# Reordering the branch units of a one-core Strassen block: pool, pool, conv, conv, then by turns

## The chip, the cores and the metric

The kernel runs on one core of one Trainium2 chip. The metric is the device time of one execution in microseconds (us), measured over several runs; times are compared by the median. The engines are TensorE (PE, matrix products; PEld are its weight loads), VectorE (DVE), ScalarE (ACT), GpSimd (POOL, which here only issues DMAs and adds by DMA) and SyncE (SP, which issues the loads of the weights).

## The reference

One decoder block over 256 tokens and 4096 channels, in float32. The input is normed and projected by one large matrix; the parts feed a pooling branch and a gated short convolution; both results `ys` (2048 channels each) go through a matrix of their own to 4096 channels, are gated and added, and go through an output matrix.

```python
h = rmsnorm(x, norm_w[l])
proj = jnp.einsum('bsd,de->bse', h, w_in[l])
u_p, z_p, u_c, b_c, c_c, z_c, g_logit = jnp.split(proj, SPLIT_POINTS, axis=-1)
y_pool = causal_multiscale_pool(u_p, pool_w[l], pool_scale[l]) * jax.nn.silu(z_p)
y_conv = causal_gated_shortconv(u_c, b_c, c_c, conv_w[l], conv_b[l]) * jax.nn.silu(z_c)
ys = jnp.stack([y_pool, y_conv], axis=2)
br = jnp.einsum('bsnc,ncd->bsnd', ys, w_branch[l])
gates = jax.nn.sigmoid(g_logit.reshape(b, s, N_BRANCHES, d) + gate_b[l])
merged = jnp.sum(gates * br, axis=2)
x = x + jnp.einsum('bsd,de->bse', merged, w_out[l])
return rmsnorm(x, final_norm_w)
```

## The kernel before

**Units and steps.** The work is a list of units. A unit makes 1024 output columns for all 256 tokens, and works through its input channels in steps of 256 channels. Every operand is split into a high and a low float32r part, and a product is three matmuls: high by high, high by low, low by high. A step is plain (`P`: eight products, 24 matmuls of 128x512) or a Strassen-like step (`S`: seven products, 21 matmuls). The text of a unit, such as `PPPPSSPS`, names its steps in order. Units named `b0_c` and `b1_c` (c from 0 to 3) are the branch units: b0 takes the pooling branch, b1 the convolution, c is the block of 1024 output columns, eight steps each. They come after the gate units (`g1_0` is the last of these) and ahead of the output units `o0` to `o3`.

**Weights.** A step's weights are one load of 1 MB by SP into one of three `raw` buffers; a buffer is loaded again when the step that held it has been prepared. ACT rounds `raw` into the high parts in `ring`, DVE subtracts to make the low parts (`ring<-raw`). For an `S` step DVE also makes four sums in `parts`, which ACT and DVE split the same way (`ring<-parts`). The ring has 15 cells of 512 columns; a plain step takes 4, an `S` step 3 and then 4 more. PE gives a cell back when its products are done. Work is written out up to four steps ahead of PE, three at the end of a unit that is marked urgent, and each engine runs its instructions in the order in which they are written.

**Banks.** Four PSUM banks (`sums`) hold the output quarters and four more (`shared`) the corners of the `S` steps. When a bank has its last matmul, ACT empties it: `sums` into `E`, `shared` into `J`. DVE combines the corners in `J` and adds them to `E` (`E<-E,J`). In a unit that is marked `late`, POOL adds them instead by two accumulating DMAs (`gather`, E<-J). In a plain last step the `sums` banks close in its second half; in a closing `S` step they close in its first nine matmuls, and one in the step before.

**What follows a unit.** `epi` returns a list of actions, of which one is written out per tick, a tick being six matmuls of PE; `gap(n)` is n empty ticks. For `b0_c` the result in `E` is multiplied by its gate in `Y` (`Y<-E,Y`). For `b1_c` `E` is multiplied by the gate in the tile `last_pair`, which `spare()` returns (`gated`), then the product of the first branch is added; PE transposes the sum into `shared`, ACT copies it, and POOL stores it in `m_d[c]` (`put`). `Y` then takes the next gate from `gates_d`. The first two gates are never stored: `g0_0` lies in `Y`, `g1_0` in `last_pair`.

**Fills.** The operands of the branch units (`y_ops`) come from DRAM (`y_d`) through three staging tiles `sa`, `sb`, `sc`, into `arena`: POOL fetches, DVE makes four small sums for an `S` operand, ACT writes the high part, DVE the low (`arena<-sa` and so on). They start in the last gate unit, first all of b0 in the order of its steps, then all of b1; the output units' operands follow from `m_d` in the same way, each once its c has been stored.

Lines 58 and 61 of the profile are the helpers for ACT and DVE, 82 and 85 those of POOL's DMAs, 1026 the matmuls of steps and 462 the transposes.

Of the kernel before, what the change touches and what calls it, by code (L numbers as in the profile page):

```python
# [9 lines left out]
F32 = mybir.dt.float32  # L10
# [5 lines left out]
P = 128  # L16
# [3 lines left out]
NU = 1024  # L20
NH = 512
# [19 lines left out]
HOST = "PPBPPMMPSSPSSPSSPSS"  # L41
TEN = "PSPSSPSSPSSPSSPS"
OUT3 = "PSPSPSPSPSPSSPPP"
B0 = "PPPPSPSP"
B1 = "PSPSPSPP"
B1_FIRST = "PPSPSPSP"
B0_MORE = "PPPPSSPS"


@with_exitstack  # L50
def hybrid_block(ctx: ExitStack, tc: tile.TileContext, x, xc, prm, rows_in, w_in, pool_w, w_branch, w_out, out):
# [5 lines left out]
    def act(dst, src, func=AF.Copy, **kw):  # L57
        return pin(nc.scalar.activation(dst, src, func, **kw))  # L58

    def tt(dst, a, b, op):  # L60
        return pin(nc.vector.tensor_tensor(out=dst, in0=a, in1=b, op=op))  # L61

    def mul(dst, a, b):
        return tt(dst, a, b, ALU.mult)

    def add(dst, a, b):
        return tt(dst, a, b, ALU.add)
# [13 lines left out]
    def move(dst, src):  # L81
        return pin(nc.gpsimd.dma_start(dst, src))
# [8 lines left out]
    dram = ctx.enter_context(tc.tile_pool(name="dram", bufs=1, space=bass.MemoryType.DRAM))  # L91

    def sb(name, shape, dt=F32):
        return upper.tile(shape, dt, name=name)

    def blocks(name, shape, dt=F32):
        return const.tile(shape, dt, name=name)
# [4 lines left out]
    E = blocks("E", [P, 2, NU])  # L102
    sa = blocks("sa", [P, 8, P])
    J = blocks("J", [P, 4, NH])
    ident = blocks("ident", [P, P])
    raw = sb("raw", [P, NRAW, 2 * NU])
    Y = sb("Y", [P, 2, NU])
# [10 lines left out]
    gates_d = dram.tile([2, 4, P, 2, NU], F32, name="gates_d")  # L118
    g_d = dram.tile([2, P, 2, NU], F32, name="g_d")
    side_d = dram.tile([2, P, 2, 4, P], F32R, name="side_d")  # L120
    y_d = dram.tile([2, 2, P, 4, 2, T], F32, name="y_d")
    m_d = dram.tile([4, P, 4, 2, T], F32, name="m_d")
    o_d = dram.tile([3, P, 2, NU], F32, name="o_d")

# [28 lines left out]
    def open_last(dt):  # L153
        stack = ExitStack()
        ctx.enter_context(stack)
        pool = stack.enter_context(tc.tile_pool(name="last", bufs=1, side="right"))
        last_pair.update(stack=stack, tile=pool.tile([P, 8 * KB], dt, name="last_pair"))
# [87 lines left out]
    def quarters(tile_):  # L245
        return tile_.rearrange("p a (b c) -> p (a b) c", c=NH)
# [154 lines left out]
    def shared(i):  # L401
        return PF[i]
# [52 lines left out]
    def transposes(src, done):  # L455
        items = []
        for j in range(4):
            def f(j=j):
                for i in range(2):
                    for t in range(2):  # L460
                        c = (2 * j + i) * P
                        pin(nc.tensor.transpose(shared(j)[:, i * T + t * P:i * T + (t + 1) * P],  # L462
                                                src[:, t, c:c + P], ident))
                done(j)
            items.append(f)
        return items

    def pairs(items):
        return [lambda a=a, b=b: (a(), b()) for a, b in zip(items[::2], items[1::2])]

    def put(dst, src):
        for k in range(2):
            move(dst[:, :, 1 - k], src.rearrange("p (q k) t -> p q k t", k=2)[:, :, k])

    def chan(tile_):
        return tile_.rearrange("p a n -> p (a n)").rearrange("p (b t) -> p b t", t=T)

    def bankview(j):
        return shared(j).rearrange("p (b t) -> p b t", t=T)

    def gap(n):
        return [None] * n
# [36 lines left out]
    def seq_y(text):  # L519
        return sequence(text, 8 - text.count("S"), 8, 0)  # L520
# [189 lines left out]
    def spare():  # L710
        return last_pair["tile"].rearrange("p (a n) -> p a n", a=2)

    def branch_unit(n, c):
        def epi(u):
            if n == 0:
                if c:
                    return gap(10) + [lambda: move(spare(), gates_d[1, c])] + gap(8) + [lambda: mul(Y, E, Y)]
                return gap(8) + [lambda: mul(Y, E, Y)]
            turned = spare() if c < 3 else Y

            def gated():
                mul(E, E, spare())
                if c == 3:
                    last_pair["stack"].close()
                    open_last(F32R)
                    last_pair["again"] = True

            def copy(j):
                act(chan(turned)[:, 2 * j:2 * j + 2], bankview(j))

            def stored():
                put(m_d[c], chan(turned))
                merged[c] = now[0] + STORED
            return gap(2) + [gated, None, lambda: add(E, E, Y), None,
                lambda: c < 3 and move(Y, gates_d[0, c + 1])] + gap(4) + pairs(transposes(E, copy)) + [stored]

        text = (B1 if c else B1_FIRST) if n else B0_MORE if c else B0
        u = Unit(f"b{n}_{c}", lambda i: w_branch[n, c, i], seq_y(text), y_ops[n], epi)
        u.late = n == 0 and c > 0
        if not u.late:  # L740
            u.urgent, u.lead = (lambda: None), 3
        units.append(u)
# [91 lines left out]
            gate_unit(n, c)  # L834
    gate_unit(1, 0)
    last_x = units[-1]
    for c in range(4):
        branch_unit(0, c)
        branch_unit(1, c)
    for c in range(4):  # L840
        out_unit(c)

# [126 lines left out]
    def done(i):  # L969
        steps[i].prepared = True  # L970
# [184 lines left out]
    for st in lead:  # L1155
# [7 lines left out]
        if not combined and last.closed(FB):  # L1163
            combined = True
            flush()
            rest = sums.rearrange("p (t a) n -> p t (a n)", t=2)
# [80 lines left out]
```

## Time and profile before

| what | value |
|---|---|
| runs | 2356.61, 2357.35, 2359.06 us; median 2357.35 |
| profiled execution | 2356.82 us, span 2354.7 us |
| granted TensorE clock, mean | 0.999 |
| branch units, from the first to the last matmul | 1674.9 to 2014.3 us of the span |
| matmuls and transposes | 10424 |
| DMA | 569.44 MB, mean 242 GB/s |

The page counts an engine's busy time; PE's matmuls overlap in the pipeline, so that the busy time of a group is not its count times its pitch. "Idle before" is how long the engine stood ahead of an instruction, and the name behind the arrow is what ended that. In a table by windows each row is a stretch of the span, with the busy time and the number of instructions of PE, PEld, DVE, ACT and POOL, then PE's granted clock, the DMA engines' share and GB/s. In a timeline each row is a start, a duration and the work, and equal neighbours are merged.

### The profile page before, as it was taken

To read this page: it belongs to the slowest core of one execution; us is meant where nothing else is said; L and a number is where in the kernel's file an instruction comes from. 1 tells how busy PE (TensorE), PEld (TensorE's weight loads), DVE (VectorE), ACT (ScalarE), POOL (GpSimd) and SP (SyncE) were. 2 spreads that over 40 slices of the span, in tenths; PEclk is the share of its full clock that TensorE was granted. 3 is DMA by queue.
4 is the path that set the end of the run, shared out by engine and by line. 5 is a ranking of instruction groups with operands and counts; after the bars stand their busy time and mean duration, and the time that the engine had idled before them with its cause. 6 is when DMAs were issued, how large, how long until landed. Compare 5 with 4: busy or idle time off the path is not lost.

```text
span 2354.7 us, 28337 instructions
## 1 busy us (share of the span) xinstructions
PE 2340.7 (99%) x10424; PEld 1938.7 (82%) x10424; DVE 2217.8 (94%) x2454; ACT 1542.9 (66%) x1841; POOL 139.0 (6%) x195
## 2 busy tenths in 40 slices
PE   9999999999999999999999999999999999999998
PEld 7888888888888888888888888888888888888886
DVE  8899989999979979979999999998999899999998
ACT  6666756766656666666677767677666566566664
POOL 0000000000001000100000000001101001000000
PEclk9999999999999999999999999999999999999999
DMA  9667655776656656656787787778767678767877
GB/s 351 231 234 248 217 201 215 251 232 233 222 207 216 219 196 213 220 198 222 242 258 254 256 265 246 250 267 283 258 225 247 254 247 282 250 206 263 260 255 279
DMA packets 95387, 569.44 MB, mean 242 GB/s; under 512 B 10320, under 2 KB 10576, under 8 KB 34832
## 3 DMA queue, kind: packets, MB, share of 16 engines
q1 hardware_dynamic: 69824, 485.39, 56.7%
q0 software_dynamic: 24848, 81.01, 13.7%
q8 instruction: 81, 1.33, 0.2%
q10 hardware_dynamic: 576, 1.24, 0.1%
q14 instruction: 58, 0.48, 0.1%
HBM read 521.46 MB, written 25.17 MB: 232 GB/s over the span
## 4 chain that ended last, share of the span: by engine, by line
PE 97%; DVE 1%; DMA 0%; ACT 0%; issue 0%; DVEq 0%; SPq 0%; ACTq 0%
PE sums L1026 70%; PE shared L1026 25%; PE shared L676 1%; PE shared L462 1%; DVE ring L61 1%; DMA raw<-in_w_branch_dram 0%; DVE parts L61 0%; DMA raw<-in_w_in_dram 0%; ACT ring L58 0%; DVE arena L61 0%; PE shared L652 0%; DVE J L61 0%; ACT E L58 0%; PE shared L653 0%; PE shared L655 0%
## 5 line engine op out<-in xcount | busy, mean ns | idle before, releaser
L1026 PE MATMUL sums<-ring,arena 128*128 128x512 f32 x7011 | 1640.7, 390 | 1.9 <-ACT E L58 1.1
L1026 PEld LDWEIGHTS sums<-ring,arena 128*128 128x128 f32 x7011 | 1315.3, 188 | 275.5 <-ACT E L58 1.5
L61 DVE TENSOR_TENSOR ring<-raw,ring 128x1024 fp32r<-128x1024 f32 (+2 forms) x887 | 962.2, 1104 | 70.4 <-ACT ring L58 69.5
L58 ACT ACTIVATE ring<-raw 128x1024 fp32r<-128x1024 f32 (+3 forms) x682 | 785.5, 1192 | 210.2 <-PE sums L1026 98.5
L58 ACT ACTIVATE ring<-parts 128x512 fp32r<-128x512 f32 (+1 forms) x683 | 510.4, 761 | 510.2 <-DVE parts L61 438.3
L1026 PE MATMUL shared<-ring,arena 128*128 128x512 f32 x2241 | 541.1, 389 | 0.0
L61 DVE TENSOR_TENSOR ring<-parts,ring 128x1024 fp32r<-128x1024 f32 (+1 forms) x475 | 524.5, 1146 | 8.7 <-ACT ring L58 8.7
L1026 PEld LDWEIGHTS shared<-ring,arena 128*128 128x128 f32 x2241 | 420.6, 188 | 87.3
L61 DVE TENSOR_TENSOR parts<-parts,raw 128x512 f32<-128x512 f32 x444 | 303.3, 683 | 0.0
L61 DVE TENSOR_TENSOR parts<-raw 128x1024 f32<-128x1024 f32 x222 | 270.2, 1217 | 10.9 <-DMA raw<-in_w_in_dram 6.0
L61 DVE TENSOR_TENSOR J<-J 128x512 f32<-128x512 f32 (+1 forms) x90 | 78.1, 868 | 6.0 <-ACT J L58 2.8
L1026 PE MATMUL sums<-ring,last_pair 128*128 128x512 f32 x306 | 76.2, 389 | 0.0
L58 ACT ACTIVATE J<-shared 128x512 f32<-128x512 f32 x128 | 69.5, 601 | 1.6
L1026 PEld LDWEIGHTS sums<-ring,last_pair 128*128 128x128 f32 x306 | 57.4, 188 | 11.9
L85 POOL DMA_DIRECT2D E<-J x28 | 34.2, 1463 | 479.5 <-ACT ring L58 300.1
L1026 PE MATMUL shared<-ring,last_pair 128*128 128x512 f32 x216 | 51.9, 389 | 0.0
L1026 PE MATMUL shared<-ring,side 128*128 128x512 f32 x207 | 50.7, 389 | 0.0
L1026 PEld LDWEIGHTS shared<-ring,last_pair 128*128 128x128 f32 x216 | 40.5, 188 | 8.4
L1026 PEld LDWEIGHTS shared<-ring,side 128*128 128x128 f32 x207 | 38.9, 188 | 8.1
L58 ACT ACTIVATE E<-sums 128x512 f32<-128x512 f32 x76 | 41.8, 592 | 4.5 <-PE sums L1026 2.7
L85 POOL DMA_DIRECT2D Y<-J x12 | 14.7, 1458 | 265.1 <-ACT ring L58 138.5
L58 ACT ACTIVATE E<-sums,rin 128x512 f32<-128x512 f32 x20 | 13.0, 689 | 13.9 <-PE sums L1026 13.9
(140 smaller groups left out, 645.6 us busy)
## 6 DMA issues: line engine op xcount, KB each, us to landing
raw<-in_w_in_dram SPq DMA_DIRECT2D x318, 1024.0 KB, 4.9
raw<-in_w_branch_dram SPq DMA_DIRECT2D x64, 1024.0 KB, 5.4
raw<-in_w_out_dram SPq DMA_DIRECT2D x64, 1024.0 KB, 4.8
E<-J POOLq DMA_DIRECT2D x28, 512.0 KB, 8.6
E<-in_rows_dram POOLq DMA_DIRECT2D x14, 512.0 KB, 9.8
Y<-J POOLq DMA_DIRECT2D x12, 512.0 KB, 9.3
gates_d<-E POOLq DMA_DIRECT2D x6, 1024.0 KB, 6.1
y_d<-E POOLq DMA_DIRECT2D x8, 512.0 KB, 5.2
```

The source lines that it names most:

```text
L58: return pin(nc.scalar.activation(dst, src, func, **kw))
L61: return pin(nc.vector.tensor_tensor(out=dst, in0=a, in1=b, op=op))
L85: return pin(nc.gpsimd.dma_start(dst, src, accum_op=ALU.add))
L462: pin(nc.tensor.transpose(shared(j)[:, i * T + t * P:i * T + (t + 1) * P], src[:, t, c:c + P], ident))
L676: pin(nc.tensor.matmul(o, a, b, start=(k, i) == (0, 0), stop=(k, i) == (3, 2)))
L1026: pin(nc.tensor.matmul(ps, lhs, rhs, start=n == 0, stop=n == u.total[b] - 1))
```

## The change

The order of the branch units was b0_0, b1_0, b0_1, b1_1, and so on by turns. Now it is b0_0, b0_1, b1_0, b1_1, and from c = 2 by turns. Two products of the first branch then wait at the same time, and there is one `Y`: the first goes to DRAM (`p_d`), `Y` takes the gate of the second, and after b1_0 the first comes back into `J`, where it is added. `last_pair` gets the gate of b1_1 only after m_d[0] has been stored from it.

All b0 units have the text `PPPPSSPS` and are late. b0_0 had `PPPPSPSP` and was not late. b1_0 had `PPSPSPSP` and now has `PSPSPSPP`, as all b1 units but b1_1, which has `PPPPSSSP`.

```diff
-B0 = "PPPPSPSP"
 B1 = "PSPSPSPP"
-B1_FIRST = "PPSPSPSP"
-B0_MORE = "PPPPSSPS"
+B_LATE = "PPPPSSPS"
+B1_SECOND = "PPPPSSSP"
...
+    p_d = dram.tile([P, 2, NU], F32, name="p_d")
...
             if n == 0:
-                if c:
-                    return gap(10) + [lambda: move(spare(), gates_d[1, c])] + gap(8) + [lambda: mul(Y, E, Y)]
-                return gap(8) + [lambda: mul(Y, E, Y)]
+                product = gap(18) + [lambda: mul(Y, E, Y)]
+                if c == 0:
+                    return product + [None, lambda: move(p_d, Y), lambda: move(Y, gates_d[0, 1])]
+                if c > 1:
+                    product[10] = lambda: move(spare(), gates_d[1, c])
+                return product
...
-            return gap(2) + [gated, None, lambda: add(E, E, Y), None,
-                lambda: c < 3 and move(Y, gates_d[0, c + 1])] + gap(4) + pairs(transposes(E, copy)) + [stored]
-
-        text = (B1 if c else B1_FIRST) if n else B0_MORE if c else B0
+            head = gap(2) + [gated, None, lambda: add(E, E, Y), None,
+                             lambda: c < 3 and move(Y, gates_d[0, c + 1])] + gap(4)
+            rest = []
+            if c == 0:
+                head = [lambda: move(J, p_d.rearrange("p a (b n) -> p (a b) n", n=NH)), None, gated] + gap(4) + [
+                    lambda: add(quarters(E), quarters(E), J)] + gap(3)
+                rest = gap(7) + [lambda: move(spare(), gates_d[1, 1])]
+            return head + pairs(transposes(E, copy)) + [stored] + rest
+
+        text = B_LATE if n == 0 else B1_SECOND if c == 1 else B1
         u = Unit(f"b{n}_{c}", lambda i: w_branch[n, c, i], seq_y(text), y_ops[n], epi)
-        u.late = n == 0 and c > 0
+        u.late = n == 0
...
-    for c in range(4):
-        branch_unit(0, c)
-        branch_unit(1, c)
+    for n, c in ((0, 0), (0, 1), (1, 0), (1, 1), (0, 2), (1, 2), (0, 3), (1, 3)):
+        branch_unit(n, c)
```

The instructions of an engine stand in a fixed order. Three places of it matter below.

DVE in the second half of b0_0, before: the lows and sums for the seventh step (`S`) and the lows of the last one (`P`), with pieces of fills between.

```order
L61 TENSOR_TENSOR parts<-raw 128x1024
L61 TENSOR_TENSOR ring<-raw,ring 128x512
L61 TENSOR_TENSOR parts<-parts,raw 128x512
L61 TENSOR_TENSOR ring<-raw,ring 128x2x512
L61 TENSOR_TENSOR parts<-parts,raw 128x512
L61 TENSOR_TENSOR arena<-sb,arena 128x1024
L61 TENSOR_TENSOR ring<-parts,ring 128x2x512 x2
L61 TENSOR_TENSOR arena<-sc,arena 128x512
L61 TENSOR_TENSOR ring<-raw,ring 128x2x512 x2
L61 TENSOR_TENSOR sa<-sa 128x128 x4
L61 TENSOR_TENSOR ring<-raw,ring 128x4x512
```

The same place now: the last lows of the sixth step, the lows of the seventh (`P`), and then all of the last one, which is an `S`.

```order
L60 TENSOR_TENSOR arena<-sa,arena 128x1024
L60 TENSOR_TENSOR ring<-parts,ring 128x2x512
L60 TENSOR_TENSOR ring<-parts,ring 128x512 x2
L60 TENSOR_TENSOR ring<-raw,ring 128x2x512 x2
L60 TENSOR_TENSOR arena<-sb,arena 128x512
L60 TENSOR_TENSOR sc<-sc 128x128 x4
L60 TENSOR_TENSOR parts<-raw 128x1024
L60 TENSOR_TENSOR ring<-raw,ring 128x512
L60 TENSOR_TENSOR parts<-parts,raw 128x512
L60 TENSOR_TENSOR ring<-raw,ring 128x2x512
L60 TENSOR_TENSOR parts<-parts,raw 128x512
L60 TENSOR_TENSOR ring<-parts,ring 128x2x512 x2
```

Where one plain step was being prepared stands a Strassen step; the fills between are of about the same size.

POOL from the last fetches of `y_d` on, before:

```order
L82 DMA sc<-y_d 128x512
L82 DMA sa<-y_d 128x512
L82 DMA Y<-gates_d 128x2048
L82 DMA m_d<-last_pair 512x1x256 x2
L82 DMA sa<-m_d 128x512
L82 DMA sb<-m_d 128x512
L82 DMA sc<-m_d 128x512
L85 DMA E<-J 128x2x512 x2
L82 DMA last_pair<-gates_d 128x2048
```

And now:

```order
L81 DMA sc<-y_d 128x512
L81 DMA sa<-y_d 128x512
L84 DMA E<-J 128x2x512 x2
L81 DMA p_d<-Y 128x2048
L81 DMA Y<-gates_d 128x2048
L84 DMA E<-J 128x2x512 x2
L81 DMA J<-p_d 128x2048
L81 DMA m_d<-last_pair 512x1x256 x2
L81 DMA sa<-m_d 128x512
L81 DMA sb<-m_d 128x512
L81 DMA last_pair<-gates_d 128x2048
```

Two adding DMAs for b0_0, the store of `p_d` and the load from it are new; the first store into `m_d` stands behind them.

DVE after b1_0, before: the corners are added to `E`, then the gate is applied, and the product in `Y` is added between the sums of a Strassen step and their lows.

```order
L61 TENSOR_TENSOR E<-E,J 128x2048
L61 TENSOR_TENSOR ring<-raw,ring 128x4x512
L61 TENSOR_TENSOR E<-E,last_pair 128x2048
L61 TENSOR_TENSOR parts<-raw 128x1024
L61 TENSOR_TENSOR ring<-raw,ring 128x512
L61 TENSOR_TENSOR parts<-parts,raw 128x512
L61 TENSOR_TENSOR ring<-raw,ring 128x2x512
L61 TENSOR_TENSOR parts<-parts,raw 128x512
L61 TENSOR_TENSOR E<-E,Y 128x2048
L61 TENSOR_TENSOR ring<-parts,ring 128x2x512 x2
```

And now, in b1_1, which follows b1_0:

```order
L60 TENSOR_TENSOR E<-E,J 128x2048
L60 TENSOR_TENSOR ring<-raw,ring 128x4x512
L60 TENSOR_TENSOR E<-E,last_pair 128x2048
L60 TENSOR_TENSOR parts<-raw 128x1024
L60 TENSOR_TENSOR ring<-raw,ring 128x512
L60 TENSOR_TENSOR parts<-parts,raw 128x512
L60 TENSOR_TENSOR ring<-raw,ring 128x2x512
L60 TENSOR_TENSOR parts<-parts,raw 128x512
L60 TENSOR_TENSOR E<-E,J 128x2048
L60 TENSOR_TENSOR ring<-parts,ring 128x2x512 x2
```

The product is added at the same place, from `J` in place of `Y`; the second `E<-E,J` is the one that reads what came back from `p_d`. PE's transposes of `E` stand 69 matmuls into the unit that follows b1_0, as before.

## The prediction

> **What bounds the kernel now.** I read the page first, then what TensorE (PE) waited for, then the branch stage by windows, then the timelines at the places that the change touches. PE does 99% of the span and 97% of the chain that ended last.
>
> ```profile
> span 2354.7 us, 28337 instructions
> ...
> PE 2340.7 (99%) x10424; PEld 1938.7 (82%) x10424; DVE 2217.8 (94%) x2454; ACT 1542.9 (66%) x1841; POOL 139.0 (6%) x195
> ...
> PE 97%; DVE 1%; DMA 0%; ACT 0%; issue 0%; DVEq 0%; SPq 0%; ACTq 0%
> ```
>
> A busy PE could still be a slow PE, so the pitch of the matmuls is wanted: in the first row below 26 matmuls start between 1769.70 and 1775.60 (the next row's start), 0.227 us each. The waits of PE come to 3.0 us in three places, two of them at the very start of the program. The third lies in the stage that is changed.
>
> ```profile
> 1769.70 6.06 PE L1026 MATMUL sums<-ring,arena 128*128 128x512 f32 x26
> 1775.60 1.03 PE L462 MATMUL shared<-ident,E 128*128 128x128 f32 x8
> ...
> PE shared L873 <- DVE warm L869: 1.1, 1, 1.1
> PE sums L1026 <- ACT E L58: 1.1, 1, 1.1
> PE sums L1026 <- DVE ring L774: 0.8, 1, 0.8
> ```
>
> The four windows below are the first four branch units (b0_0, b1_0, b0_1, b1_1). Only the first loses PE time. VectorE (DVE) is nearly full in the first two, where the operands of both branches are still being filled, and has room in the next two.
>
> ```profile
> 1674.90:1718.30 43.40, 42.33 (x188) 34.72 (x186) 41.67 (x51) 31.21 (x39) 5.06 (x8) 1.00 0.80 263
> 1718.30:1760.00 41.70, 41.70 (x184) 34.51 (x185) 40.74 (x44) 27.32 (x34) 0.00 (x0) 1.00 0.55 202
> 1760.00:1803.20 43.20, 43.20 (x200) 35.95 (x199) 39.45 (x38) 26.24 (x32) 3.64 (x6) 1.00 0.71 255
> 1803.20:1844.70 41.50, 41.50 (x184) 34.36 (x184) 37.67 (x35) 27.14 (x32) 3.05 (x3) 1.00 0.75 255
> ```
>
> So a gain is bounded: PE cannot run ahead of its own matmuls, and there is one wait to take away. What is open is whether DVE, which feeds PE, is still in time.
>
> **The change part by part.**
>
> *One Strassen step more in the first unit.* A plain step is 24 matmuls, a Strassen step 21. Before, b0_0 holds two of them, now three; every other unit keeps three. Three matmuls fewer at 0.227 us: -0.7 us, straight on PE.
>
> *The wait at the end of b0_0.* It comes from ScalarE (ACT):
>
> ```profile
> 1710.95 6.28 PE L1026 MATMUL sums<-ring,arena 128*128 128x512 f32 x27
> 1718.30 1.90 PE L1026 MATMUL sums<-ring,arena 128*128 128x512 f32 x7 [1.07 <-ACT E L58]
> ...
> 1715.76 1.49 ACT L58 ACTIVATE ring<-raw 128x1536 fp32r<-128x1536 f32 x1 [1.29 <-DMA raw<-in_w_branch_dram]
> 1717.15 0.61 ACT L58 ACTIVATE arena<-sb 128x512 fp32r<-128x512 f32 x1
> 1717.67 2.04 ACT L58 ACTIVATE E<-sums 128x512 f32<-128x512 f32 x4
> ```
>
> After 27 matmuls from 1710.95 the next was due at 1717.08 and came at 1718.30: 1.2 us, and 0.1 more in the slower start of the second row. ACT stood at the rounding of a weight tile that had not landed, and the emptying of the sums banks was queued behind it. The unit ended with a plain step, whose banks close in the last 2.7 us. Now it ends with a Strassen step, which closes one bank in the step before and the others in its first nine matmuls, as b0_1 does before, at whose end (1803.20) the windows show no loss. -1.3 us. This is gone unless DVE is late there, which is the next term.
>
> *DVE in b0_0.* The rows are those of before, from the first sum of its fifth step:
>
> ```profile
> 1687.48 1.21 DVE L61 TENSOR_TENSOR parts<-raw 128x1024 f32<-128x1024 f32 x1
> ...
> 1691.56 1.22 DVE L61 TENSOR_TENSOR arena<-sc,arena 128x1024 fp32r<-128x1024 f32 x1
> 1692.69 2.35 DVE L61 TENSOR_TENSOR ring<-parts,ring 128x1024 fp32r<-128x1024 f32 x2
> 1694.97 0.68 DVE L61 TENSOR_TENSOR arena<-sa,arena 128x512 fp32r<-128x512 f32 x1
> 1695.57 1.01 DVE L61 TENSOR_TENSOR sb<-sb 128x128 f32<-128x128 f32 x4
> 1696.50 2.35 DVE L61 TENSOR_TENSOR ring<-raw,ring 128x1024 fp32r<-128x1024 f32 x2
> 1698.77 1.22 DVE L61 TENSOR_TENSOR parts<-raw 128x1024 f32<-128x1024 f32 x1
> ...
> 1698.03 2.88 PE L1026 MATMUL shared<-ring,arena 128*128 128x512 f32 x12
> ```
>
> By start to start: the five sums and lows of a Strassen step 1691.56 - 1687.48 = 4.08, its last two lows 2.28, a plain step's lows 2.27, fills 1.13 (1024 wide), 0.60 (512), four small sums 0.93; a fill 896 wide lies between, I take 1.0. In the new order, from the same 1687.48: sums 4.08 (1691.56), three fill pieces 1.0 + 0.60 + 0.93 (1694.09), lows 2.28 (1696.37), the next step's sums 4.08 (1700.45), a fill 1.13 (1701.58), lows in three pieces, about 2.34 (1703.92), a plain step 2.27 (1706.19), 0.60 + 0.93 (1707.72), the last step's sums 4.08 (1711.80) and lows 2.28 (1714.08). PE: the fifth step starts six matmuls before 1698.03, at 1696.67; then 21, 21 and 24 matmuls bring the last step to 1711.65. Its third group (in a closing step N4, on the last of the four summed cells) needs its low part seven matmuls in, at 1713.24. DVE is 0.85 us late there, +0.85; up to there it is in time, by 0.5 us at the narrowest. Bounds: 0 if the fills run shorter, and 0.85 + 1.7 = 2.6 if DVE also idles as it did in that window (43.40 - 41.67). I take 0.85: the rows of before had hardly any idle time inside this stretch.
>
> *After it.* The fills of the second branch (five of the eight still stand here) and the sums of b0_0 now lie beside b0_1, which has four plain steps first. Summed the same way, DVE ends the lows of b0_1's last step about 1.5 us before PE needs them. +0.1, bounds 0 and 2.6 - 1.5 = 1.1.
>
> *E by way of DMA in b0_0.* Its corner sums are now added by two accumulating DMAs and not by DVE. That takes one 2.29 us add from DVE and puts two transfers into b0_1, 9.5 us each by the median in the fence after the next paragraph, 19 us if one followed the other; their reader, the product Y<-E,Y, stands 18 ticks of six matmuls, 24.5 us, behind. Hidden by b0_1's own matmuls: 0.
>
> *Y to p_d and back.* After that product POOL stores Y and, once it has landed, loads the next gate into Y. Behind these two on POOL's queue stand only the adding DMAs of b0_1, due at the end of the unit; two transfers of some 6 us fit. No PE work waits for them: 0. Back comes the product into J, and here something does wait. These rows of before show the same place one unit pair on (b1_1 to b0_2, unit start 1844.7):
>
> ```profile
> 1845.56 2.29 DVE L61 TENSOR_TENSOR E<-E,J 128x2048 f32<-128x2048 f32 x1 [0.46 <-ACT E L58]
> 1856.73 2.28 DVE L61 TENSOR_TENSOR E<-E,Y 128x2048 f32<-128x2048 f32 x1
> 1860.38 1.03 PE L462 MATMUL shared<-ident,E 128*128 128x128 f32 x8
> 1859.33 0.56 POOL L82 DMA_DIRECT2D Y<-gates_d  x1 [47.35 <-DVE E L61]
> ...
> raw<-in_w_branch_dram SPq DMA_DIRECT2D x35, 1024.0 KB, 5.5
> Y<-gates_d POOLq DMA_DIRECT2D x3, 1024.0 KB, 5.6
> E<-J POOLq DMA_DIRECT2D x4, 512.0 KB, 9.5
> last_pair<-gates_d POOLq DMA_DIRECT2D x2, 1024.0 KB, 17.6
> ```
>
> J may be loaded once E<-E,J has read it, at +3.1; issue took 0.3 us more for Y (1859.33 against 1859.01). With 5.6 us J lands at +9.1. The adding of J has the place that E<-E,Y had, +12.0, and PE's transposes come at +15.7. So 2.9 us of room at the add, and 4.2 us (15.7 - 9.1 - 2.3 for the add is 4.3, less the semaphores) until PE stands: 0. Bound above: 17.6 us, the same size behind two adding DMAs; it is the rival below. I take 5.6, since the two DMAs ahead of J landed long before.
> [...]
>
> *Three Strassen steps in a row in b1_1.* The ring of 15 cells lets a third step (7 cells) in only as the first gives its cells back, so DVE cannot work far ahead; but the four plain steps before leave it in front. At the end of b1_1 a plain step closes the banks late again, with three weight tiles of the next unit emitted ahead of the emptying: the pattern of the old wait. Bounds 0 (the end of b1_1 in before, 1844.70) and 1.3 (the end of b0_0 in before). DVE frees the weight tile earlier than in b0_0, without fills: I take 0.3.
>
> *Later units.* The cells of the ring shift by three, and the transposes come three matmuls later; both only move pieces: 0.
>
> Sum: -0.7 - 1.3 + 0.85 + 0.1 + 0.3 = -0.75 us. The profiled execution took 2356.82 us (span 2354.7 and 2.1 around it), 0.53 below the median 2357.35; so 2356.1 for its like, and 2356.6 as a median.
>
> **The rivals.**
>
> *A. Everything is covered.* The two gains stand alone: 2357.35 - 2.0 = 2355.35. For it: b0_1 to b1_3 of before ran with no PE wait at all. Against: DVE is 96% full in the very window that gets 4.1 us more DVE work (6.36 for a Strassen step against 2.27).
>
> *B. DVE is the bound through the first two units.* The upper bounds together: -2.0 + 2.6 + 1.1 + 1.3 = +3.0, 2360.35. For it: the windows at 41.67 and 40.74 busy. Against: PE needs 183 matmuls per unit and the fills that are left for the second unit stand beside four plain steps in a row.
>
> *C. J comes late (the other side).* The transposes of E stand in PE's order behind the add of J. From a landing time of about 9.9 us (4.3 more than 5.6) on, each further us is one of PE. At 17.6 us, J lands at +21.0, the add ends at +23.4, PE stands 7.7 us: 2356.6 + 7.7 = 2364.3, slower by 0.3%; it passes the 4.7 us line at a landing of some 15.4 us. For it: the 17.6 us row, for the same size on the same queue. Against: that row stood behind E<-J, and nothing stands ahead of J here.
> [...]
>
> *D. The order is not what it says.* The instruction order shows all three moves and one Strassen step more; the time would be 2357.35. Hardly open.
>
> **How the numbers follow.** Forecast (one small wait in b0_0, the rest hidden) 0.55; A 0.20; B 0.14; C 0.08; D and others 0.03. 0.2% is 4.7 us, about what a measurement of this kernel can tell from no change. The forecast, A, B and D lie within it. Faster by more would need a gain over the 2.0 us that PE has to give: 0.02. Slower: C and a B beyond its bound, 0.09. Same: 0.89. The range reaches from A, less 0.4 for the scatter of runs (the runs of before lie between 2356.61 and 2359.06), to B: 2355.0 to 2360.3.
>
> **What would show it.** In the changed profile: no ACT wait of PE at the end of b0_0; instead, if anything, about a us in its last step, released by DVE's ring lows. J<-p_d landing 5 to 7 us after its issue, the second E<-E,J of DVE without idle time before it, and the transposes of b1_1 without a wait. A PE stop at those transposes would be C; PE waits spread over b0_0 and b0_1 would be B; a PE wait on ACT at the end of b1_1 above 1 us would make the 0.3 wrong.

## The result, and the profile after

The changed kernel took 2360.59 us (median of 20 runs, 2359.86 to 2363.72) against 2357.15 us for the kernel before in the same session (20 runs, 2355.99 to 2360.21). The ratio is 1.0016, 95% interval [1.0010, 1.0022]: 3.4 us slower, where 0.75 us faster was forecast, and just outside the range. The profiled execution took 2361.99 us, 1.4 above its median; the last section takes that up. One execution each of e4_tick, e6_text_only, e10_two_s_lead2 and e12_j_twice took more than 3000 us, in the slow state, and is left out of the medians below.

The page of the changed kernel answers to the first fence of the prediction: span, TensorE's busy time, and the shares of the chain that ended last.

```profile
span 2360.3 us, 28353 instructions
...
PE 2341.0 (99%) x10421; PEld 1937.3 (82%) x10421; DVE 2220.6 (94%) x2460; ACT 1543.6 (65%) x1845; POOL 142.4 (6%) x199
...
PE 97%; DMA 1%; DVE 1%; ACT 0%; issue 0%; SPq 0%; DVEq 0%; ACTq 0%
```

The three matmuls are gone (10421 for 10424), but the span is 5.6 us longer. What PE waited for, over the whole execution:

```profile
PE sums L1034 <- ACT E L57: 3.0, 2, 1.9
PE sums L1034 <- DVE ring L60: 2.1, 2, 1.8
...
PE sums L1034 <- DVE arena L60: 1.1, 1, 1.1
```

The two rows left out, and the 1.8 of the second, stand at the program's start. In the branch units PE now waits twice for ScalarE's emptying of `E` (once before) and once for `ring` (the 0.3 that is left of that row), and in the output unit o0 once for `arena`. By windows, the first and the fourth unit in their new order (b0_0 and b1_1):

```profile
1675.20:1718.57 43.37, 41.99 (x185) 34.10 (x183) 41.61 (x55) 29.35 (x36) 4.36 (x7) 1.00 0.68 224
...
1801.96:1847.33 45.37, 43.46 (x201) 35.82 (x199) 38.01 (x33) 26.40 (x30) 4.23 (x7) 1.00 0.73 266
```

The first unit loses 1.4 us, the fourth 1.9; the two between them lose nothing. There are four places to look at.

**The last step of b0_0 and its end.** PE's timeline, and below it ScalarE's over the same place:

```profile
1707.63 6.05 PE L1034 MATMUL sums<-ring,arena 128*128 128x512 f32 x26
1714.00 0.74 PE L1034 MATMUL sums<-ring,arena 128*128 128x512 f32 x2 [0.32 <-DVE ring L60]
1714.58 2.93 PE L1034 MATMUL shared<-ring,arena 128*128 128x512 f32 x12
1718.57 3.77 PE L1034 MATMUL sums<-ring,arena 128*128 128x512 f32 x14 [1.06 <-ACT E L57]
```

```profile
1713.15 2.08 ACT L57 ACTIVATE ring<-raw 128x1024 fp32r<-128x1024 f32 x3
1715.13 0.62 ACT L57 ACTIVATE arena<-sa 128x512 fp32r<-128x512 f32 x1
1715.65 0.58 ACT L57 ACTIVATE E<-sums 128x512 f32<-128x512 f32 x1
1716.13 1.90 ACT L57 ACTIVATE ring<-raw 128x2048 fp32r<-128x2048 f32 x1
1717.94 1.55 ACT L57 ACTIVATE E<-sums 128x512 f32<-128x512 f32 x3
```

From 1707.63 and 26 pitches of 0.227 the next matmul was due at 1713.53 and came at 1714.00: VectorE was late with a low part. From 1714.58 and 12 pitches b0_1 was due at 1717.30 and came at 1718.57. ScalarE had emptied one `sums` bank at 1715.65, then rounded a whole weight tile for b0_1 (1.90 us), and only then emptied the other three.

**The end of b1_1.** PE, ScalarE and the DMAs from 1828 to 1848 (count, size, median us from issue to landing):

```profile
1839.14 6.28 PE L1034 MATMUL sums<-ring,arena 128*128 128x512 f32 x27
1847.33 8.92 PE L1034 MATMUL sums<-ring,arena 128*128 128x512 f32 x31 [1.91 <-ACT E L57]
```

```profile
1840.17 1.92 ACT L57 ACTIVATE ring<-raw 128x2048 fp32r<-128x2048 f32 x1 [1.59 <-DMA raw<-in_w_branch_dram]
1841.99 1.06 ACT L57 ACTIVATE J<-shared 128x512 f32<-128x512 f32 x2
1844.88 1.91 ACT L57 ACTIVATE ring<-raw 128x2048 fp32r<-128x2048 f32 x1 [1.82 <-DMA raw<-in_w_branch_dram]
1846.70 2.04 ACT L57 ACTIVATE E<-sums 128x512 f32<-128x512 f32 x4
```

```profile
raw<-in_w_branch_dram SPq DMA_DIRECT2D x4, 1024.0 KB, 7.9
last_pair<-gates_d POOLq DMA_DIRECT2D x1, 1024.0 KB, 10.9
...
sc<-m_d POOLq DMA_DIRECT2D x1, 256.0 KB, 12.3
```

b0_2 was due at 1839.14 + 27 x 0.227 = 1845.26 and came at 1847.33: 2.07 us. ScalarE stood at the rounding of b0_2's third weight tile, whose load had not landed, with the emptying of all four banks queued behind it. The loads, 5.5 us by the median before, took 7.9 here, beside four fetches by POOL. Of the 31 matmuls that follow, eight near the start stand 0.427 us apart in place of 0.227, which is another 1.6 us.

**The last step of o0.** PE and VectorE:

```profile
2098.94 0.61 PE L1034 MATMUL sums<-ring,arena 128*128 128x512 f32 x2
2100.62 1.88 PE L1034 MATMUL sums<-ring,arena 128*128 128x512 f32 x7 [1.06 <-DVE arena L60]
```

```profile
2099.48 1.08 DVE L60 TENSOR_TENSOR arena<-sa,arena 128x896 fp32r<-128x896 f32 x1
```

VectorE writes the last piece of the step's own operand at 2099.48 to 2100.56; PE was due at 2098.94 + 2 x 0.227 = 2099.39.

**The way by DRAM.** The tile `J` and the add that reads it:

```profile
L81 POOL DMA_DIRECT2D J<-p_d x1: 567/567/567, 1805.4 to 1805.4; - x1
...
DMA to landing us min/median/max: 5.1/5.1/5.1
```

```profile
1813.96 2.29 DVE L60 TENSOR_TENSOR E<-E,J 128x2048 f32<-128x2048 f32 x1
...
1817.61 1.03 PE L462 MATMUL shared<-ident,E 128*128 128x128 f32 x8
```

Issued at 1805.39, landed at 1810.46, read at 1813.96 without idle time ahead of the add; the transposes come at 1817.61 without a wait.

The table sums what PE lost against its pitch of 0.227 us at each place, read from the starts of its matmuls, for this and for the kernels of the next section (from b0_0 on; the start of o0, at most 0.32 us, and losses below 0.3 are left out; "end of the second unit" is where b1_0 ends in the old order). Slow matmuls are in the number. The transposes in b0_2 have no column; e8_all and e10_two_s_lead2 lose about 0.5 there.

| kernel | in b0_0 | end of b0_0 | b0_1 | end of the second unit | transposes in b1_1 | end of b1_1 | end of o0 | o2 |
|---|---|---|---|---|---|---|---|---|
| before | | 1.35 | | | | | | 0.31 |
| after | 0.59 | 1.62 | | | | 3.77 | 1.33 | |
| e1_lead2 | 0.58 | 1.67 | | | | | 1.32 | |
| e2_fetch_later | 0.58 | 1.67 | | | | | 1.32 | |
| e3_sss_pp | 0.58 | 1.66 | | | 2.4 | 0.49 | 1.32 | |
| e4_tick | 0.58 | 1.67 | | | | 4.52 | | 0.59 |
| e5_limit | 0.59 | | 1.73 and 1.68 | | | 1.59 | 1.34 | |
| e6_text_only | | 1.58 | | 2.20 | | | 1.34 | |
| e7_two_s | | | | | | 4.15 | | |
| e8_all | 0.59 | | 1.70 and 0.53 | | | | | 0.40 |
| e9_j_late | 0.59 | 1.62 | | | | 2.30 | 1.34 | |
| e10_two_s_lead2 | | | | | | | | |
| e11_before_held | | | | 1.49 | | | | |
| e12_j_twice | 0.58 | 1.65 | | | 1.2 | 3.90 | 1.33 | |

For the changed kernel: 7.31 less the 1.66 of before, less 0.68 for the three matmuls, is 5.0; with 0.24 at the start of o0 and 0.3 by which b0_0 begins later that is 5.5 of the span's 5.6.

### The profile page after: what moved, and what is told of

It is laid out like the page before. It is cut to its first block, busy times and chain, and to the rows that moved or that the text cites. A ratio compares the mean times of both kernels' runs of the same rounds, so it can differ in the third digit from the quotient of the medians.

```text
span 2360.3 us, 28353 instructions
## 1 busy us (share of the span) xinstructions
PE 2341.0 (99%) x10421; PEld 1937.3 (82%) x10421; DVE 2220.6 (94%) x2460; ACT 1543.6 (65%) x1845; POOL 142.4 (6%) x199
## 3 DMA queue, kind: packets, MB, share of 16 engines
q8 instruction: 81, 1.33, 0.2%
## 4 chain that ended last, share of the span: by engine, by line
PE 97%; DMA 1%; DVE 1%; ACT 0%; issue 0%; SPq 0%; DVEq 0%; ACTq 0%
PE sums L1034 70%; PE shared L1034 25%; PE shared L676 1%; PE shared L462 1%; DMA raw<-in_w_in_dram 1%; DVE ring L60 0%; DMA raw<-in_w_branch_dram 0%; ACT ring L57 0%; PE shared L652 0%; PE shared L653 0%; PE shared L655 0%; ACT E L57 0%; ACT arena L57 0%; SPq L75 0%; DVE parts L60 0%
## 5 line engine op out<-in xcount | busy, mean ns | idle before, releaser
L60 DVE TENSOR_TENSOR parts<-parts,raw 128x512 f32<-128x512 f32 x446 | 308.5, 692 | 0.0
```

## The experiments

Each edit is against the changed kernel unless it says otherwise.

### Two tiles ahead at the end of b1_1

```diff
-            u.urgent, u.lead = (lambda: None), 3
+            u.urgent, u.lead = (lambda: None), 2 if c == 1 else 3
```

> At the end of b1_1 (the fourth unit) two weight tiles of the next unit are rounded by ACT ahead of the emptying of the sums banks, not three. Theory Q (the emptying is queued on ACT behind the rounding of the third tile, whose load lands late): the PE stop of 2.07 us between b1_1 and b0_2 goes, and with it the eight matmuls at 0.427 us that follow it (1.6 us in the changed kernel's profile): 2 to 3.7 us faster than the changed kernel, about 2357.5. Rival S (three Strassen steps in a row leave DVE and ACT behind as a whole): the stop stays at 1 us or more, because the banks or the next tiles are late anyway, and the time stays within 1 us of the changed kernel.

2358.45 us (before: 2356.76; ratio 1.0008, [0.9999, 1.0017]), span 2356.2. ScalarE and PE at the end of b1_1:

```profile
1843.11 2.64 ACT L57 ACTIVATE E<-sums 128x512 f32<-128x512 f32 x4 [1.57 <-PE sums L1034]
```

```profile
1838.83 13.54 PE L1034 MATMUL sums<-ring,arena 128*128 128x512 f32 x59
```

ScalarE now waits for the banks and not for a load, with the third tile behind the emptying, and 59 matmuls run through. The stop and the slow matmuls are gone, all else is unchanged. The order in ScalarE's queue is a necessary condition of that stop.

### The fetches for o0 later

```diff
-                merged[c] = now[0] + STORED
+                merged[c] = now[0] + STORED + (24 if c == 0 else 0)
```

> The three fetches from m_d[0] that follow its store are issued 24 ticks later, so that they no longer share the DMA engines with the loads of the weights in the last third of b1_1; the load of the gate into last_pair stays. Theory D (the third tile is late because its load shares the engines with these fetches: 8.5 us against 4.7 us undisturbed): the load takes 5 to 6.5 us and the stop between b1_1 and b0_2 shrinks by 2 us or more, to nothing. Rival R (the raw buffer is free too late, whatever the load takes): the stop shrinks by less than 1 us.

2358.41 us (ratio 1.0007, [0.9998, 1.0016]), span 2356.5. The weight loads of the same window, and ScalarE's third tile, which keeps its place ahead of the emptying:

```profile
raw<-in_w_branch_dram SPq DMA_DIRECT2D x4, 1024.0 KB, 5.1
```

```profile
1842.38 1.92 ACT L57 ACTIVATE ring<-raw 128x2048 fp32r<-128x2048 f32 x1
1844.18 2.06 ACT L57 ACTIVATE E<-sums 128x512 f32<-128x512 f32 x4
```

Without the three fetches of `m_d` beside them the loads take 5.1 us in place of 7.9, ScalarE no longer waits, and the stop is gone as well. So it took both: a tile ahead of the emptying, and a load that POOL's fetches made late. Either mend alone is enough.

### The three Strassen steps one place earlier in b1_1

```diff
-B1_SECOND = "PPPPSSSP"
+B1_SECOND = "PPPSSSPP"
```

> b1_1 has its three Strassen steps still in a row, but one place earlier (PPPSSSPP). Theory E (what matters is that a Strassen step stands just before the closing plain step, so that the raw buffers and ring cells for the next unit come free late): the stop between b1_1 and b0_2 goes, as at the end of b1_1 before; 2 to 3.7 us faster than the changed kernel, unless the transposes, which now stand beside the first of the three, cost up to 1 us. Rival S (three in a row are the cause): a stop of 1 us or more stays, there or inside the three steps.

2362.51 us (ratio 1.0023, [1.0014, 1.0033]). The stop at the end shrinks to 0.49, but there is a new one among PE's waits, and VectorE's add, in its timeline, shows why:

```profile
PE shared L462 <- DVE E L60: 2.2, 1, 2.2
```

```profile
1818.14 2.28 DVE L60 TENSOR_TENSOR E<-E,J 128x2048 f32<-128x2048 f32 x1
```

The sums of the second Strassen step now come ahead of the adding of `J` in VectorE's order; `J` was issued at 1805.9 and with the 5.1 us of above had landed at about 1811, but the add ran from 1818.14 to 1820.42, and PE's transposes waited for it. The time in which VectorE adds `J` is set by its own queue, not by the transfer. Two plain steps at the end shrink one stop by making another.

### One half tick more

```diff
     for u in units:
+        if u.name == "b0_1":
+            state["mm"] += 3
```

> The count that makes the ticks gets three more at the start of b0_1, so that all later actions fall at the same matmul of their unit as before the change. Theory T (the three matmuls that the first unit lost shift every later tick; by that the last fill of o0 slid behind the lows of one more step): the PE stop of 1.2 us before the last step of o0 goes, about 1.3 us faster than the changed kernel. Rival F (the fills are late because m_d[0] is stored one unit pair later): the stop stays.

2361.44 us (ratio 1.0017, [1.0008, 1.0026]). The three counts put the ticks back where they stood against the matmuls in the kernel before. The stop at the end of o0 is gone, and the one at the start of o0 (0.24) too; in their place the end of b1_1 grew to 4.52 and 0.59 turned up in o2. That the o0 stop comes from the shift of the ticks by three matmuls is shown; moving them back is no gain.

### The second tile of b0_1 held back

```diff
         if u.urgent and st is u.steps[-1]:
             state["limit"] = state["now"] + u.lead
+        if u.name == "b0_0" and st in u.steps[-2:]:
+            state["limit"] = state["now"] + (1 if st is u.steps[-1] else 2)
```

> The changed kernel with one number held back: in the last two steps of b0_0 the preparation of b0_1's weights may run only one tile ahead, so that ScalarE's rounding of the second tile (1.90 us) no longer stands ahead of the emptying of the shared banks. Theory Q (the 1.62 us stop between b0_0 and b0_1 is the order of ScalarE's queue): that stop falls to 0 to 0.3 us, the 3.8 us at the end of b1_1 and the 1.3 us in the fourth piece's last step stay, the time is 1.3 to 1.6 us below the changed kernel's 2360.6, about 2359.1. Rival theory (the stop is only paid elsewhere: VectorE is late in the last step of b0_0, and the tile that is held back is missed by the first step of b0_1): a stop of 1 us or more turns up inside b0_1, and the time stays at 2360.2 to 2360.8.

2361.77 us (before: 2357.05; ratio 1.0023, [1.0013, 1.0033]). b0_1 starts at 1717.32, as the first theory has it, and stops one matmul into its second step; PE's rows, and VectorE's behind the emptied `J`:

```profile
1717.32 5.83 PE L1034 MATMUL sums<-ring,arena 128*128 128x512 f32 x25
1724.61 3.70 PE L1034 MATMUL sums<-ring,arena 128*128 128x512 f32 x15 [1.46 <-DVE ring L60]
```

```profile
1719.67 2.68 DVE L60 TENSOR_TENSOR J<-J 128x512 f32<-128x512 f32 x3 [0.48 <-ACT J L57]
1722.27 6.69 DVE L60 TENSOR_TENSOR ring<-raw,ring 128x2048 fp32r<-128x2048 f32 x3
```

Four emptyings of `E` and four of `J` now stand ahead of the tile on ScalarE, and the combining of `J` ahead of its low part on VectorE; three low parts then run back to back, and PE waits 1.73 for the first of them and 1.68 again in the last step of b0_1. The stop between the units was indeed ScalarE's order, and the rival was right that it is only paid elsewhere, and more than once: 3.41 us in the place of 1.62.

### The text of the first unit alone, in the kernel before

```diff
-        text = (B1 if c else B1_FIRST) if n else B0_MORE if c else B0
+        text = (B1 if c else B1_FIRST) if n else B0_MORE
...
-        u.late = n == 0 and c > 0
+        u.late = n == 0
```

(and the product 18 ticks behind in place of 8, as in the change)

> The kernel before, with its old order of units, and only the first unit's three Strassen steps and their late start taken over from the change. Theory L (the stops in and behind the first unit come from three Strassen steps in it, whatever the order of units): a stop of about 0.6 us in its last step and of about 1.6 us behind it, less 0.7 us for the step that has 7 products in the place of 8, against the 1.35 us that stood there before: time 0 to 0.5 us above the kernel before's 2356.8; nothing at the end of the later branch units. Rival theory O (the stops come from the order, since with it b0_1 follows b0_0): no stop above 0.3 us in the last step of the first unit, and a time 0.7 us below the kernel before.

2359.80 us (before: 2357.05; ratio 1.0015, [1.0005, 1.0025]), span 2357.4, with the old order of units and no transfer by DRAM. PE, and ScalarE ahead of the second stop:

```profile
1717.21 12.83 PE L1026 MATMUL sums<-ring,arena 128*128 128x512 f32 x54 [1.02 <-ACT E L58]
...
1753.00 6.28 PE L1026 MATMUL sums<-ring,arena 128*128 128x512 f32 x27
1761.22 4.16 PE L1026 MATMUL sums<-ring,arena 128*128 128x512 f32 x17 [1.93 <-ACT E L58]
```

```profile
1758.77 1.91 ACT L58 ACTIVATE ring<-raw 128x2048 fp32r<-128x2048 f32 x1 [3.38 <-DMA raw<-in_w_branch_dram]
```

Both theories miss. The stop inside b0_0 is not there, but the one behind it is (1.58), a new one of 2.20 stands at the end of b1_0, where ScalarE waited 3.38 us for a load ahead of the emptying, and the one at the end of o0 is the same as in the changed kernel. The loss of the first unit's text, 2.75 us by the medians, is most of what the whole change loses (3.44), though not at all of the same places.

### Two Strassen steps in the first unit

```diff
-        text = B_LATE if n == 0 else B1_SECOND if c == 1 else B1
+        text = "PPPPSPSP" if (n, c) == (0, 0) else B_LATE if n == 0 else B1_SECOND if c == 1 else B1
```

> The changed kernel with two Strassen steps in the first unit in the place of three, still late in it. Theory L: the stop of 0.59 us in the unit's last step goes (0 to 0.2), the 1.62 us behind it stays or shrinks to about 1.3, and 0.7 us of matmuls come back: time within 0.5 us of the changed kernel's 2360.6. Rival (the third Strassen step costs nothing and only saves its 0.7 us): 2361.3.

2359.72 us (ratio 1.0013, [1.0004, 1.0022]), span 2358.2. The windows of the first two units:

```profile
1675.25:1717.41 42.16, 42.16 (x187) 34.80 (x186) 40.69 (x50) 30.98 (x38) 5.07 (x8) 1.00 0.76 248
1717.41:1758.94 41.53, 41.53 (x184) 34.38 (x184) 39.21 (x42) 26.34 (x32) 3.60 (x4) 1.00 0.81 282
```

PE loses nothing in either (42.16 of 42.16, 41.53 of 41.53): the text with the third Strassen step cost 2.2 us and saved 0.68, and the stop in o0 went with it, since the three matmuls are back. The edit also ends the unit with a plain step again; whether the number of Strassen steps or the place of the last one counts, no run separates. The median is only 0.9 below the changed kernel's: the profile here, which lies near its median, has slow matmuls at the end of b1_1 (4.15), and the profile of the changed kernel that lies near its median (e9_j_late below) has none (2.30). This is the new order of units with the way by DRAM and the old number of steps, and it removes even the stop that the kernel before has behind b0_0. What is left is that end, 4.15 here.

### All mends together

The edits of the first, second, fourth and fifth experiment at once.

> The changed kernel with all the mends together: preparation two tiles ahead in b1_1, the second product's fetches later, one tick more in b0_1, and the held-back tile at the end of b0_0. If the stops are independent of each other (theory I), what is left is the 0.6 us in the first unit and some tenths: span about 2353, time 2354.5 to 2356, which is 0.5 to 2 us below the kernel before. If mending one brings another (theory M: the pieces of VectorE's and ScalarE's work slide against the units each time that a tick is moved, as the one tick alone did), a stop of 1 us or more turns up at a place where the changed kernel has none, and the time is 2356.5 to 2359.

2358.05 us (ratio 1.0005, [0.9996, 1.0013]), span 2356.4. The numbers are theory M's: the ends of b1_1 and of o0 stay mended, but the held-back tile brings 1.70 in b0_1 along and the half tick 0.40 in o2. Both had done so alone (1.73 in e5_limit, 0.59 in e4_tick), so this does not show that mending one place disturbs another mend.

### J later, a miss

```diff
-                head = [lambda: move(J, p_d.rearrange("p a (b n) -> p (a b) n", n=NH)), None, gated] + gap(4) + [
+                head = gap(2) + [gated, None, lambda: move(J, p_d.rearrange("p a (b n) -> p (a b) n", n=NH))] + gap(2) + [
```

> The changed kernel with the load of J from p_d issued four ticks (24 matmuls, 5.4 us) later; nothing else is moved. In the changed kernel J landed at 1810.46 and its reader, the add into E, started at 1813.96: 3.5 us of room, and the transposes behind it started at 1817.61, 1.4 us after the add's end at 1816.25. Theory R (the round trip is free because of this room): J lands at about 1815.9, the add waits about 1.9 us on the DMA and ends at about 1818.2, so TensorE stops about 0.6 us at the transposes; VectorE, which is held up 1.9 us there, may be late for one more step in b1_1: time 0.6 to 2.5 us above the changed kernel's 2360.6. Rival (the load may land at any time, since VectorE's order around the add has slack): no stop at the transposes, time within 0.4 us of 2360.6.

2360.31 us (before: 2356.66; ratio 1.0015, [1.0006, 1.0024]). The edit did nothing: POOL had no other work, so that a later place in the list of actions left its order as it was, and the DMA was issued at 1805.51 as soon as VectorE had read `J`. The order of instructions is that of the changed kernel on every engine, so this is a second profile of the changed kernel, and is used as such below. A tick sets an order, not a time.

### Two Strassen steps, and two tiles ahead in b1_1

The edits of e7_two_s and e1_lead2.

> The changed kernel with two Strassen steps in the first unit, which ran without any stop in the first four units, and two tiles ahead in the place of three at the end of b1_1, which took that stop away. Theory I (the two mends are independent): no stop of TensorE above 0.4 us is left in the branch units or the fourth piece, span 2354.0 to 2354.4, time 2355.7 to 2356.3, that is 0.7 to 1.4 us below the kernel before's 2357.05. Rival theory M (each mend slides the fills against the steps, and another stop turns up): a stop of 1 us or more at another place, time 2356.8 to 2358.5.

2356.34 us against 2356.66 for the kernel before (ratio 0.9997, [0.9988, 1.0006]). What PE waited for from 400 to 2300 us:

```profile
PE shared L462 <- DVE E L60: 0.3, 1, 0.3
```

No stop but this one, at the transposes in b0_2, is left in the whole changed stage; these two mends are independent. The time is just above the range of the first theory (2355.7 to 2356.3): the median is 0.3 below the kernel before, which cannot be told from no change. In the profiles the matmuls from the start of b0_0 to the last one take 667.2 us, against 668.4 in the kernel before; the profiled execution of this kernel began b0_0 2.6 us later (1677.45 for 1674.90) and ended 0.6 us later behind its last matmul. The new order is no slower than the old, with next to nothing lost in its stage; that is all it has to give at the same number of matmuls.

### A held-back tile in the kernel before

```diff
         if u.urgent and st is u.steps[-1]:
             state["limit"] = state["now"] + u.lead
+        if u.name == "b0_0" and st in u.steps[-2:]:
+            state["limit"] = state["now"] + (2 if st is u.steps[-1] else 3)
```

> The kernel before, with one number held back: at the end of b0_0 the next unit's third tile (a Strassen step's) is rounded behind the emptying of the shared banks and not ahead of it. Theory Q (ScalarE's queue order alone made the kernel before's one stop of 1.35 us): the stop goes, time 1.0 to 1.4 us below the kernel before, about 2355.8. Rival (VectorE is the real limit of the first two units there too, and the held-back Strassen step comes late): a stop of 0.8 us or more, released by VectorE, in b1_0 or at its end; time within 0.5 us of the kernel before or above it.

2357.87 us against 2356.66 (ratio 1.0005, [0.9997, 1.0014]). b1_0 starts on time at 1717.06, but the stop is 43 us further on, at the end of b1_0 (1.49 us), where ScalarE now waits for a load ahead of the emptying:

```profile
1757.58 2.01 ACT L58 ACTIVATE ring<-raw 128x1024 fp32r<-128x1024 f32 x2 [1.49 <-DMA raw<-in_w_branch_dram]
```

The kernel before's stop is of the same kind, and taking it away there gains nothing: PE comes 1.2 us earlier and meets a load that does not come earlier.

### J loaded twice

```diff
-                head = [lambda: move(J, p_d.rearrange("p a (b n) -> p (a b) n", n=NH)), None, gated] + gap(4) + [
+                head = [lambda: move(J, p_d.rearrange("p a (b n) -> p (a b) n", n=NH)), lambda: move(J, p_d.rearrange("p a (b n) -> p (a b) n", n=NH)), gated] + gap(4) + [
```

> The changed kernel with the load of J from p_d issued twice, one behind the other on POOL's queue; the add reads J after the second, which carries the same data. The earlier try to delay this load moved only its place on a queue that was empty, so that it was issued at the same time, 1805.51. Theory R (the round trip is free because J lands 3.5 us ahead of its reader): if the second load waits for the first, J lands at about 1815.5 to 1816, the add (due at 1813.96) starts about 1.8 us late and ends at about 1818.1, and TensorE, whose transposes were due at 1817.61, stops 0.4 to 0.8 us; time 0.4 to 1.5 us above the 2360.3 to 2360.6 of the changed kernel. If both run side by side, J lands at about 1813 and nothing moves. Rival (a late J costs far more, since VectorE's sums and lows for the next Strassen step stand behind the add and the ring is empty): a further stop of over 1 us inside b1_1, time 2362 or more.

2363.24 us (before: 2356.75; ratio 1.0026, [1.0016, 1.0036]), span 2361.3. VectorE's add and PE's transposes:

```profile
1816.07 2.29 DVE L60 TENSOR_TENSOR E<-E,J 128x2048 f32<-128x2048 f32 x1 [2.30 <-DMA J<-p_d]
```

```profile
1799.64 17.84 PE L1034 MATMUL sums<-ring,arena 128*128 128x512 f32 x78
1818.41 1.09 PE L462 MATMUL shared<-ident,E 128*128 128x128 f32 x8 [0.93 <-DVE E L60]
```

The second load waited for the first, and the data came 10.9 us after the first issue (1805.11 to 1816.0). Rival C of the prediction had each us beyond 9.9 cost one of PE: 1.0, and PE waited 0.93 (1.2 in the table). Nothing else moved in the places of the table. The median, though, is 2.6 above the changed kernel's, beyond the range of theory R and where the rival had it, but the rival's further stop inside b1_1 is not in the trace. The profiled execution here lies near its median and has slow matmuls at the end of b1_1; that of the changed kernel which lies near its median (e9_j_late) has none, and the spans of these two differ by 2.4 us: about 1.2 for `J`, 1.6 for the slow matmuls, less 0.4 by which this one began earlier. How often either kernel has slow matmuls no run counts.

## Why the prediction was wrong, point by point

- *One Strassen step more, -0.7:* right as far as it goes, 0.68 on PE.
- *The wait at the end of b0_0, "-1.3 us. This is gone unless DVE is late there":* wrong, the first failed step. 1.62 stands there. When the banks close was read rightly (one bank was emptied at 1715.65, ahead of the unit's end), but not what stands between the emptyings on ScalarE: 1.90 us of rounding. b0_1 of before, whose end showed no loss, was taken as the likeness, and its ScalarE rows were not read. In them no tile stands between the emptyings:

```profile
1798.78 2.56 ACT L58 ACTIVATE E<-sums 128x512 f32<-128x512 f32 x4
```

That this order is the cause is shown by e5_limit, and so is that holding this tile back does not pay. What removes the stop is the text with two Strassen steps and a plain end (e7_two_s). The term was 1.6 us off.

- *DVE in the last step of b0_0, +0.85:* right in place and releaser, 0.59. *After it, +0.1:* right, nothing in the changed kernel; but e5_limit shows that the stop itself had made the room: with it gone, VectorE is late twice.
- *E by DMA, Y to p_d, J back, 0:* right; 5.1 us from issue to landing against 5.6 taken, and e12_j_twice confirms where the room ends. The 5.1 us fell into a unit in which VectorE was busy 38.01 of 45.37 us.
- *Three Strassen steps in b1_1, +0.3, bounds 0 and 1.3:* wrong, the second failed step and the largest. The pattern was named (three tiles ahead of the emptying), and it was then sized by VectorE, which frees the tile in time. The late party is the load. The POOL fetches for o0, which the order of before has in b0_1 and which now come with the store of `m_d[0]` into the end of b1_1, stand in the rows of POOL's order that the part on the change shows, and no term priced them; they stretched the loads from 5.1 to 7.9 us (e2_fetch_later). The stop is 2.07 and 2.19 us in the two profiles of the changed kernel, against a bound of 1.3, and 1.6 more where the clock dropped; the prediction had named a wait above 1 us there as the sign that this term is wrong.
- *Later units, "both only move pieces: 0":* wrong, the third failed step. Three matmuls fewer shift the ticks by half of one, and in o0 a piece of fill slid behind two low parts: 1.33. e4_tick, which puts the three counts back, and e7_two_s, which puts the matmuls back, do not have it; e6_text_only, which lacks them in the old order of units, has it.
- *The rivals:* B's time, 2360.35, is close to the one measured, but by chance: its places were VectorE's in the first two units (0.59 of the 3.7 that it put there), and ScalarE and the loads did the rest. C and D did not happen. What did is a drop of PE's clock, to 0.50 behind the stop at the end of b1_1, for which the sum had no term.

Of the profile of before the sum did not use ScalarE's idle time on `raw<-in_w_branch_dram`, which it had quoted once; it is the tell-tale at the end of b1_1 (1.82) and at those stops of e6_text_only and e11_before_held (3.38 and 1.49), though not at the end of b0_0, where the rounding waited for no load.

## What to carry to other kernels

Ahead of a unit's end, list what stands in front of each emptying in the queue of the engine that does it, and when the load behind each of those instructions lands; a prefetch ahead of an emptying is free only while its load is early and its own time (1.90 us at the end of b0_0) still fits before the bank is needed. When a change moves fetches, price them against the loads that they meet (7.9 us by the median at the end of b1_1, 5.1 without the three fetches), not only by their own readers. In a kernel whose order is planned by counting matmuls, three matmuls fewer are a change of order in all that follows, and mending one place moves the next: of seven mends tried one by one here, three held (two tiles ahead, fetches later, two Strassen steps in the first unit), and four brought a stop elsewhere.

## What the runs showed of the hardware

PE's matmuls slowed behind some stops of about 2 us and not behind others. In the changed kernel the matmuls behind the 2.07 us stop at the end of b1_1 start 0.427 us apart seven times in a row; e9_j_late, with the same order of instructions, stopped a little longer at the same place and went on at 0.227. Its row, which ends at 1856.25 as the changed kernel's does:

```profile
1847.57 8.68 PE L1034 MATMUL sums<-ring,arena 128*128 128x512 f32 x37 [2.03 <-ACT E L57]
```

37 matmuls there, 31 in the changed kernel's row above. Such slow matmuls stand behind stops in the profiles of the changed kernel, e4_tick, e7_two_s and e12_j_twice (2.1, 2.8, 2.4 and 2.2 us), and not behind those of e5_limit, e6_text_only, e9_j_late and e3_sss_pp (1.6, 2.1, 2.2 and 2.4 us). They cost 1.6 us, about what the changed kernel's profile lies above its median, and the spans of the two profiles, 2360.3 and 2358.9, differ by 1.4.

In the changed kernel the granted clock was half from 1847.45 to 1850.87. By windows (it is the third figure from the end):

```profile
1844.04:1847.45 3.41, 1.50 (x8) 0.92 (x7) 3.34 (x5) 2.57 (x3) 0.00 (x0) 1.00 0.92 324
1847.45:1850.87 3.42, 3.42 (x9) 2.65 (x10) 3.42 (x2) 3.29 (x5) 0.00 (x0) 0.50 0.56 204
```

The stop from 1845.26 to 1847.33 lies in the first of them, where the clock was 1.00. What tells the two cases apart is not shown: slow matmuls came behind stops of 2.1 to 2.8 us in four profiles and not behind stops of 1.6 to 2.4 us in four others, so that much the same stop costs 1.6 us in one execution and not in the next.

The weight loads at the end of b1_1 took 5.1 us by the median in e2_fetch_later and 7.9 in the changed kernel, with three more transfers of 256 KB by POOL under way; and a load of 1 MB by POOL took 5.1 us without those (`J`, and 5.0 for `last_pair` in e2_fetch_later) and 10.9 beside them.
